# Low parts of every second unit of the down weights: an adding DMA in place of a subtraction on VectorE

## The chip, the core and the metric

The kernel runs on one core of one Trainium2 chip. The metric is the device time of one launch in microseconds (us). The kernel before takes 1096.26 us, the median of 3 runs (1096.07 to 1096.92).

Engines are named as the profile names them: PE is TensorE (matmuls; PEld is its weight load), DVE is VectorE, ACT is ScalarE, POOL is GpSimd, SP is SyncE, which here only issues DMAs.

## The reference

One encoder layer over 256 tokens of width 2048, all in float32. The change touches only its last product:

```
h = RMSNorm(x) ; p = h @ w_in                      # [256, 2048] @ [2048, 4640]
x = x + concat(attention, gated linear attention) @ w_out
u = DWConv3(RMSNorm(x) @ w_up)                     # [256, 2048] @ [2048, 11264]
x = x + (silu(u[:, :5632]) * u[:, 5632:]) @ w_down # [256, 5632] @ [5632, 2048]
```

## The kernel before, in words

Every large product is done in three passes, so that a matmul of the type float32r (a float32 that is rounded as ACT or DVE writes it) gives nearly float32 accuracy. Each operand is split in two parts: a high part `hi`, which is the operand rounded, and a low part `lo`, which is the operand less `hi`. The product is hi\*hi + hi\*lo + lo\*hi, accumulated in one PSUM bank.

Weights come in units of 512 KB, [128 partitions, 1024 columns], each of which holds two k-tiles of 512 columns in the down projection. For each unit the helper `weights` (L102 to L110) does three things: SP issues the load of the raw unit `r` (L104), ACT copies it into `hi`, rounded (L108), and DVE writes `lo = r - hi` (L109). In the down projection (L653 to L669) there are four column chunks `c` of 512 columns and in each 22 units `u`, so 88 units. A unit feeds 12 matmuls of 128x512: for two k-tiles and two tiles of tokens, `a`\*`wh` (L667), `a`\*`wl` (L668) and `b`\*`wh` (L669), where `a` and `b` are the parts of the gated activations and `wh`, `wl` are the parts of the weights. Only L668 reads the low part.

The tiles rotate through pools: 4 buffers of `raw`, 4 of `hi`, 3 of `lo`. A unit can only write into a buffer when the unit that had it last is done with it: `lo` of unit n waits for the last L668 of unit n-3, `hi` of unit n for the last L669 of unit n-4, and the load of raw unit n for the subtraction (and the copy) of unit n-4. In the profile the tiles of the down stage are named `rd`, `hd` and `ld`, and its PSUM banks `pd`.

Each engine runs its own instructions in one fixed order. A scheduler makes this order when the kernel is built, from the order of the code and a priority (`tc.high_priority`) which pulls the splits ahead; an instruction that waits holds up all that stand behind it on its engine.

Of the kernel before, what the change touches and what calls it, by code (L numbers as in the profile page):

```python
# [9 lines left out]
F32R = mybir.dt.float32r  # L10
BF16 = mybir.dt.bfloat16
U32 = mybir.dt.uint32
AF = mybir.ActivationFunctionType
ALU = mybir.AluOpType
# [3 lines left out]
A = slice(None)  # L18
P = 128
T = 256  # L20
# [7 lines left out]
EPS = 1e-6  # L28
WCOLS = 1024

# Column chunks of the input projection: (name, [(first column, width), ...], whole width).
IN_CHUNKS = [
    ("kv", [(1024, 512)], 512),
    ("qa0", [(0, 512)], 512),
# [9 lines left out]


def in_units(ci):
    """k-tiles of each weight unit of a chunk of the input projection."""
    return [1] * 4 + [2] * 6 if ci == 0 else [3] * 5 + [1] if ci in (3, 4) else [2] * 8


# Small constants and parameters, by column.
C_COS, C_SIN, C_MASK, C_MF, C_MB = 0, 256, 512, 1024, 1280
C_QG, C_QGS, C_KG, C_KGS = 1536, 1664, 1792, 1920
NCST = 2048
# [5 lines left out]
def tile_hymba_layer(  # L60
# [15 lines left out]
    nc = tc.nc  # L76
    V, S, G, PE = nc.vector, nc.scalar, nc.gpsimd, nc.tensor
# [3 lines left out]
    wp = ctx.enter_context(tc.tile_pool(name="wp", bufs=3))  # L81
# [20 lines left out]
    def weights(flat, first, cols, name):  # L102
# [6 lines left out]
            V.tensor_tensor(lo[:, :cols], r[:, :cols], hi[:, :cols].bitcast(F32), ALU.subtract)  # L109
        return hi, lo  # L110

    def split(hi, lo, src):
        S.activation(hi, src, AF.Copy)
        V.tensor_tensor(lo, src, hi.bitcast(F32), ALU.subtract)

    def product(d, a, b, start=True, stop=True):
        """d (+)= a^T b, of operands in two parts each."""
        PE.matmul(d, a[0], b[0], start=start, stop=False)
        PE.matmul(d, a[0], b[1], start=False, stop=False)
        PE.matmul(d, a[1], b[0], start=False, stop=stop)  # L120
# [1 line left out]
    def both(tiles, *index):  # L122
        return [x[index] for x in tiles]

# [1 line left out]
    g1 = pers.tile([P, NKT], F32, name="g1")  # L126
    nc.scalar.dma_start(out=g1, in_=n1)
    prm_sb = pers.tile([P, NPRM], F32, name="prm_sb")
# [11 lines left out]
        hl.append(arena([P, 8, T], F32R, f"hl{i}"))  # L140

    def load_x(kt, n):
        """n k-tiles of x, scaled by the first norm's weight and split."""
        i, o = kt // 8, kt % 8
        nc.sync.dma_start(out=xts[i][:, o : o + n], in_=xt[:, kt : kt + n])
        for j in range(n):
            with tc.high_priority(offset=1500):
                S.activation(hh[i][:, o + j], xts[i][:, o + j], AF.Copy, scale=g1[:, kt + j : kt + j + 1])
                V.scalar_tensor_tensor(
                    out=hl[i][:, o + j], in0=xts[i][:, o + j], scalar=g1[:, kt + j : kt + j + 1],  # L150
                    in1=hh[i][:, o + j].bitcast(F32), op0=ALU.mult, op1=ALU.subtract,
                )
# [46 lines left out]
    def load_wa():  # L199
        nc.sync.dma_start(out=wa_sb, in_=wa)  # L200

# [1 line left out]
    in_first = [0]  # L203

    hooks = {}
# [29 lines left out]
        with tc.high_priority(offset=1500):  # L235
            S.activation(dst, src, func, scale=rstd1[:, t : t + 1])

# [1 line left out]
    rope_kg = arena([P, 2, 1024], F32, "rope_kg")  # L239
    rope = rope_kg[:, 0].rearrange("p (a b c d) -> p a b c d", a=2, b=2, c=2)  # L240
    kg_sb = rope_kg[:, 1].rearrange("p (t c) -> p t c", t=2)
# [107 lines left out]
        if h % 2 == 1:  # L349
            split(oah[:, h - 1 : h + 1], oal[:, h - 1 : h + 1], po.rearrange("p (k s) -> p k s", k=2))  # L350

# [1 line left out]
    lr_sb = pers.tile([P, 2, 32], F32, name="lr_sb")  # L353
    gkT = arena([P, 2, GH, T], F32, "gkT")
    gh = arena([P, 2, 1024], F32R, "gh")
# [59 lines left out]
                gkT[:, 1, :, t * P : t * P + P], pq.rearrange("p (h s) -> p h s", h=GH), AF.Copy, scale=float(P) ** -0.5  # L415
            )

    # The blocks of e: for a key, -F3, the levels, B3; for a query, -B3, the levels, F3. By direction and tile of
    # tokens: (first column in the bank, role, first column in e, width, sign).
    PARTS = (  # L420
# [19 lines left out]
            V.tensor_tensor(e, e, gkT[:, role, h, t * P : t * P + P].unsqueeze(1).broadcast_to([P, 4, P]), ALU.mult)  # L440

    def mix(h):
        """The decayed products of head h: A^T [s, t] over all pairs of tokens."""
        es = arena([P, 2, 2, 4, P], F32, f"es{h}")
        scaled(h, 0, es)
        yield
        scaled(h, 1, es)
        yield

        def blk(role, t, what):  # L450
            return es[:, role, t, (0, 1 + t, 2 - t, 3)[what]]

        p1 = aux(f"p1{h}")
        p2 = aux(f"p2{h}")
        for s in range(2):
            for t in range(2):
                lv = 2 if s == t else 1
                PE.matmul(p1[:, (2 * s + t) * P : (2 * s + t + 1) * P], blk(0, s, lv), blk(1, t, lv), start=True, stop=True)
        for f in range(2):
            for t in range(2):  # L460
                PE.matmul(p2[:, (2 * f + t) * P : (2 * f + t + 1) * P], blk(0, t, 3 * f), blk(1, t, 3 - 3 * f), start=True, stop=True)
        at = work([P, 4, P], F32, f"at{h}", "sc", 3)
        S.activation(at.rearrange("p a s -> p (a s)"), p1, AF.Copy)
        diag = at[:, 0::3]
        for f, c in enumerate((C_MF, C_MB)):
            V.copy_predicated(
                diag, cst_sb[:, c : c + 256].bitcast(U32).rearrange("p (a s) -> p a s", a=2),
                p2[:, 2 * f * P : (2 * f + 2) * P].rearrange("p (a s) -> p a s", a=2),
            )
        split(atr[0][:, h], atr[1][:, h], at)  # L470
# [26 lines left out]
                PE.transpose(pt[:, e * T + t * P : e * T + t * P + P], o[:, t, e * P : e * P + P], ident)  # L497
        split(ogh[:, 2 * h : 2 * h + 2], ogl[:, 2 * h : 2 * h + 2], pt.rearrange("p (k s) -> p k s", k=2))

# [1 line left out]
    def store(ci, ps):  # L501
        """What a chunk of the projection goes to."""
        for t in range(2):
            if ci >= 8:
                c = ci - 8
                d = sg[:, t, c * 512 : c * 512 + 512]
                evac(d, ps[t], t, AF.Silu)
                dv = d.rearrange("p (h e) -> p h e", h=2)
                V.tensor_tensor(dv, dv, gn.unsqueeze(1).broadcast_to([P, 2, 256]), ALU.mult)
            elif ci == 3:  # L510
                evac(lr_sb[:, t], ps[t][:, 0:32], t)
                evac(kg_sb[:, t, 0:240], ps[t][:, 32:272], t)
            else:
                evac(
                    (kv_sb[:, t], qa_sb[:, 0, t], qa_sb[:, 1, t], None, kg_sb[:, t, 240:512],
                     gq_sb[:, t], vg[:, t, 0:512], vg[:, t, 512:1024])[ci], ps[t], t,
                )
            if ci in (6, 7):
                sl = slice((ci - 6) * 512, (ci - 5) * 512)
                split(vgr[0][:, t, sl], vgr[1][:, t, sl], vg[:, t, sl])  # L520
# [1 line left out]
    running = {}  # L522

    def go(*names):
        """Emit the next stage of each of the named pieces."""
        for name in names:
            if name not in running:
                fn = {"A": attend, "Q": queries, "M": mix, "R": retrieve}.get(name[0])
                running[name] = fn(int(name[1])) if fn else {"k": keys, "g": gates, "gk": gla_keys, "gq": gla_queries}[name]()
            next(running[name], None)  # L530
# [29 lines left out]
    for ci in range(1, len(IN_CHUNKS)):  # L560
        store(ci, project(ci))

# [1 line left out]
    x1 = [arena([P, 2, 2, 512], F32, f"x1{i}") for i in range(2)]  # L564
    xs = [arena([P, 4, 2, T], F32R, f"xs{i}") for i in range(4)]
    ssq2 = pers.tile([P, 2, 4], F32, name="ssq2")
    first = 0
    for c in range(4):
# [3 lines left out]
        for u in range(NKT // 2):  # L572
            if c == 0:
                run_hooks(10, u)
            hi, lo = weights(wo, first, 1024, f"o{c}{u}")
            first += P * 1024
            for k in range(2):
                kt = 2 * u + k
                sh, sl = (oah, oal) if kt < 8 else (ogh, ogl)
                for t in range(2):  # L580
                    a = sh[:, kt % 8, t * P : t * P + P]
                    b = sl[:, kt % 8, t * P : t * P + P]
# [9 lines left out]
        for i in range(2):  # L592
            pt = aux(f"ptx{c}{i}")
            for j in range(2):
                for t in range(2):
                    n = (2 * i + j) * P
# [18 lines left out]
    rbc = pers.tile([P, T], F32, name="rbc")  # L615
    V.tensor_copy(rbc, pb[:, :T])

# [1 line left out]
    gts = [arena([P, 2, 4, T], F32R, f"g{i}") for i in range(NFF // 4)]  # L619
    first = 0  # L620
    for f in range(NFF):
# [28 lines left out]
        S.activation(gt[:, 0, f % 4], cs[1], AF.Copy)  # L650
        V.tensor_tensor(gt[:, 1, f % 4], cs[1], gt[:, 0, f % 4].bitcast(F32), ALU.subtract)

# [1 line left out]
    first = 0  # L654
    for c in range(4):
        ps = [acc(f"pd{c}{t}") for t in range(2)]
        for u in range(NFF // 2):
            hi, lo = weights(wd, first, 1024, f"d{c}{u}")
            first += P * 1024
            for k in range(2):  # L660
                kt = 2 * u + k
                gt = gts[kt // 4]
                for t in range(2):
                    a = gt[:, 0, kt % 4, t * P : t * P + P]
                    b = gt[:, 1, kt % 4, t * P : t * P + P]
                    wh, wl = hi[:, k * 512 : k * 512 + 512], lo[:, k * 512 : k * 512 + 512]
                    PE.matmul(ps[t], a, wh, start=(kt == 0), stop=False)  # L667
                    PE.matmul(ps[t], a, wl, start=False, stop=False)  # L668
                    PE.matmul(ps[t], b, wh, start=False, stop=(kt == NFF - 1))  # L669
        x1c = x1[c // 2][:, c % 2]  # L670
        for t in range(2):
            pieces = 2 if (c, t) == (3, 1) else 1
            w = 512 // pieces
            for i in range(pieces):
                sl = slice(i * w, i * w + w)
                V.tensor_tensor(x1c[:, t, sl], ps[t][:, sl], x1c[:, t, sl], ALU.add)
                q = nc.scalar if i == 0 and pieces == 2 else nc.sync
                q.dma_start(out=out[t * P : t * P + P, c * 512 + i * w : c * 512 + i * w + w], in_=x1c[:, t, sl])
# [39 lines left out]


def _units(w, sizes):  # L720
    """[K, n] -> units of a few k-tiles, each [128 partitions, k-tiles * n] in one run."""
    n, k, parts = w.shape[1], 0, []
    for per in sizes:
        parts.append(w[k : k + per * P].reshape(per, P, n).transpose(1, 0, 2).reshape(-1))
        k += per * P
    return np.concatenate(parts)
# [54 lines left out]
```

## Time and profile before

| what | value |
|---|---|
| median of 3 runs | 1096.26 us (1096.07 to 1096.92) |
| profiled execution: span from first to last instruction | 1094.4 us |
| PE busy, whole span | 1080.4 us (99%) |
| DVE busy, whole span | 783.6 us (72%) |
| ACT busy, whole span | 529.7 us (48%) |
| POOL busy, whole span | 31.2 us (3%) |
| HBM read | 199.89 MB |

The profiled execution's own time is its span of 1094.4 us; the launch adds some 1.9 us around it, if the profiled execution was like the median one (1096.26 - 1094.4). Matmuls are pipelined, so the 389 ns that the profile gives for one overlap: the next starts some 0.227 us after it. Busy shares are over the whole span; a stage is judged by rows of that stage alone. The down stage runs from about 851 us to 1090 us. The profile's line numbers are those of the kernel before; in the changed kernel all lines below L110 stand 13 lower, so that L667 to L669 are there L680 to L682.

### The profile page before, as it was taken

Reading aid. Unit: us, or ns where it says so; the run is one execution under the profiler, and the core shown is the slowest. Engines: PE = TensorE matmul, PEld = TensorE weight load, DVE = VectorE, ACT = ScalarE, POOL = GpSimd, SP = SyncE. Lnnn points to the kernel's source line nnn. Section 1 sums busy time; section 2 is a strip of 40 time slices with the busy share of each in tenths; the row PEclk is TensorE's granted clock in tenths of the full one; section 3 lists DMA queues with packets and bytes.
Section 4 is the critical chain, followed back from the end, with each engine's and each line's share of the span. In section 5 each row is a group of like instructions: output and inputs, shape, how many; then the busy total and the mean of one; then the engine's idle time right before and its main releaser. Section 6 shows DMA issues by size and latency. Waiting matters only on the chain.

```text
span 1094.4 us, 14985 instructions
## 1 busy us (share of the span) xinstructions
PE 1080.4 (99%) x5616; PEld 921.1 (84%) x5616; DVE 783.6 (72%) x1173; ACT 529.7 (48%) x780; POOL 31.2 (3%) x24
## 2 busy tenths in 40 slices
PE   7899999999999999999999999999999999999998
PEld 6789888888888888888888888888888888888886
DVE  7788777756555888888888888888888544444443
ACT  6345566764445544444444444444444433333331
POOL 4311000010000000000000000000000000000000
PEclk9999999999999999999999999999999999999999
DMA  8565544436556655655565565555565656666662
GB/s 302 173 201 165 165 154 148 139 117 187 201 194 219 200 184 184 191 186 184 189 186 184 189 187 182 190 190 179 189 191 181 195 195 210 196 214 196 210 193 79
DMA packets 58040, 202.96 MB, mean 185 GB/s; under 512 B 6576, under 2 KB 7600, under 8 KB 57840
## 3 DMA queue, kind: packets, MB, share of 16 engines
q1 hardware_dynamic: 57680, 201.87, 58.2%
q8 instruction: 44, 0.72, 0.3%
q14 instruction: 28, 0.23, 0.1%
q10 hardware_dynamic: 288, 0.14, 0.0%
HBM read 199.89 MB, written 2.10 MB: 185 GB/s over the span
## 4 chain that ended last, share of the span: by engine, by line
PE 97%; DVE 1%; DMA 1%; ACT 0%; issue 0%; SPq 0%; DVEq 0%; ACTq 0%
PE pu L632 30%; PE pu L633 15%; PE pd L667 7%; PE pd L669 7%; PE pd L668 7%; PE po L586 3%; PE po L584 3%; PE po L585 3%; PE pvg L228 1%; PE pvg L229 1%; PE pqa L229 1%; PE pgt L230 1%; PE pgt L228 1%; PE pvg L230 1%; PE pqa L230 1%; PE pgt L229 1%
## 5 line engine op out<-in xcount | busy, mean ns | idle before, releaser
L632 PE MATMUL pu<-xs,hu 128*128 128x512 f32 x1408 | 497.4, 399 | 0.0
L633 PE MATMUL pu<-xs,lu 128*128 128x256 f32 x1408 | 395.3, 281 | 0.0
L632 PEld LDWEIGHTS pu<-xs,hu 128*128 128x128 f32 x1408 | 264.4, 188 | 65.7
L108 ACT ACTIVATE hu<-ru 128x1024 fp32r<-128x1024 f32 x176 | 186.9, 1062 | 253.0 <-PE pu L632 145.6
L633 PEld LDWEIGHTS pu<-xs,lu 128*128 128x128 f32 x1408 | 266.0, 189 | 0.2
L109 DVE TENSOR_TENSOR lu<-ru,hu 128x1024 fp32r<-128x1024 f32 x176 | 215.3, 1224 | 47.4 <-PE pu L633 41.2
L109 DVE TENSOR_TENSOR ld<-rd,hd 128x1024 fp32r<-128x1024 f32 x88 | 107.8, 1225 | 117.5 <-PE pd L668 112.2
L108 ACT ACTIVATE hd<-rd 128x1024 fp32r<-128x1024 f32 x88 | 93.6, 1064 | 143.8 <-PE pd L669 136.7
L668 PE MATMUL pd<-ld,g 128*128 128x512 f32 x352 | 136.9, 389 | 0.0
L667 PE MATMUL pd<-hd,g 128*128 128x512 f32 x352 | 136.9, 389 | 0.0
L669 PE MATMUL pd<-hd,g 128*128 128x512 f32 x352 | 136.9, 389 | 0.0
L669 PEld LDWEIGHTS pd<-hd,g 128*128 128x128 f32 x352 | 66.1, 188 | 13.8
L668 PEld LDWEIGHTS pd<-ld,g 128*128 128x128 f32 x352 | 66.1, 188 | 13.6
L667 PEld LDWEIGHTS pd<-hd,g 128*128 128x128 f32 x352 | 66.1, 188 | 13.6
L109 DVE TENSOR_TENSOR lo<-ro,ho 128x1024 fp32r<-128x1024 f32 x32 | 39.0, 1224 | 36.3 <-ACT ho L108 23.8
L108 ACT ACTIVATE ho<-ro 128x1024 fp32r<-128x1024 f32 x32 | 33.9, 1061 | 44.5 <-DMA ro<-in_wo_dram 30.7
L636 DVE TENSOR_TENSOR u<-u,pu 128x256 f32<-128x256 f32 x88 | 37.0, 421 | 13.8 <-ACT u L635 13.3
L643 DVE SCALAR_TENSOR_TENSOR c<-u,prm_sb,c 128x255 f32<-128x255 f32 x88 | 42.5, 484 | 3.0
L640 DVE SCALAR_TENSOR_TENSOR c<-u,prm_sb,c 128x255 f32<-128x255 f32 x88 | 42.0, 478 | 0.1
L639 DVE TENSOR_SCALAR c<-u,prm_sb 128x256 f32<-128x256 f32 x88 | 36.2, 412 | 3.0
L637 DVE TENSOR_TENSOR u<-u,rbc 128x256 f32<-128x256 f32 x88 | 37.1, 422 | 1.5
L635 ACT ACTIVATE u<-pu 128x256 f32<-128x256 f32 x88 | 32.1, 365 | 0.0
(225 smaller groups left out, 1425.7 us busy)
## 6 DMA issues: line engine op xcount, KB each, us to landing
ru<-in_wu_dram SPq DMA_DIRECT2D x176, 512.0 KB, 3.5
rd<-in_wd_dram SPq DMA_DIRECT2D x88, 512.0 KB, 3.9
ro<-in_wo_dram SPq DMA_DIRECT2D x32, 512.0 KB, 3.6
riqa<-in_wi_dram SPq DMA_DIRECT2D x16, 512.0 KB, 4.1
rivg<-in_wi_dram SPq DMA_DIRECT2D x16, 512.0 KB, 3.5
rigt<-in_wi_dram SPq DMA_DIRECT2D x16, 512.0 KB, 3.5
riqg<-in_wi_dram SPq DMA_DIRECT2D x8, 512.0 KB, 4.0
rilk<-in_wi_dram SPq DMA_DIRECT2D x10, 408.0 KB, 3.6
```

What stands on the lines that cost most here:

```text
L108: S.activation(hi[:, :cols], r[:, :cols], AF.Copy)
L109: V.tensor_tensor(lo[:, :cols], r[:, :cols], hi[:, :cols].bitcast(F32), ALU.subtract)
L632: PE.matmul(pu, wh, x2, start=(u == 0 and k == 0), stop=False)
L633: PE.matmul(pu[:, T:], wl, x2[:, :T], start=False, stop=(u == 1 and k == 7))
L636: V.tensor_tensor(ut, ut, pu[:, :T], ALU.add)
L637: V.tensor_tensor(ut, ut, rbc, ALU.mult)
L639: V.tensor_scalar(c, ut, cw[:, 1, n : n + 1], cb[:, n : n + 1], op0=ALU.mult, op1=ALU.add)
L640: V.scalar_tensor_tensor(out=c[:, 1:T], in0=ut[:, 0 : T - 1], scalar=cw[:, 0, n : n + 1], in1=c[:, 1:T], op0=ALU.mult, op1=ALU.add)
L643: V.scalar_tensor_tensor(out=c[:, 0 : T - 1], in0=ut[:, 1:T], scalar=cw[:, 2, n : n + 1], in1=c[:, 0 : T - 1], op0=ALU.mult, op1=ALU.add)
L667: PE.matmul(ps[t], a, wh, start=(kt == 0), stop=False)
L668: PE.matmul(ps[t], a, wl, start=False, stop=False)
L669: PE.matmul(ps[t], b, wh, start=False, stop=(kt == NFF - 1))
```

## The change

Units with an even `u` go through `weights` as before. Units with an odd `u` (44 of the 88) go through a new helper, `weights_added`: the raw unit is loaded as before; ACT writes the rounded unit with its sign turned into `lo` (one more activation), and the rounded unit into `hi`; then a DMA that POOL issues reads the raw unit a second time from DRAM and adds it to what stands in `lo`. DVE does nothing for these units. The other edits of the diff drop comments and docstrings and are left out here.

```
+    def weights_added(flat, first, cols, name):
+
+        src = flat[first : first + P * cols].rearrange("(p c) -> p c", p=P)
+        r = raw(f"r{name}")
+        nc.sync.dma_start(out=r[:, :cols], in_=src)
+        hi = wp.tile([P, WCOLS], F32R, name=f"h{name}", tag="hi", bufs=4)
+        lo = wp.tile([P, WCOLS], F32R, name=f"l{name}", tag="lo")
+        with tc.high_priority(offset=1500):
+            S.activation(lo[:, :cols], r[:, :cols], AF.Copy, scale=-1.0)
+            S.activation(hi[:, :cols], r[:, :cols], AF.Copy)
+            G.dma_start(out=lo[:, :cols], in_=src, accum_op=ALU.add)
+        return hi, lo
...
-            hi, lo = weights(wd, first, 1024, f"d{c}{u}")
+            hi, lo = (weights_added if u % 2 else weights)(wd, first, 1024, f"d{c}{u}")
```

The scheduler's order changes on ACT, DVE, POOL and PE. On ACT in the middle of the first column chunk (`hd010` is the high part of chunk 0, unit 10; `ld011` the low part of unit 11; `rd` the raw units), before:

```order
L108 ACTIVATE hd010_8209<-rd010_8207 128x1024
L108 ACTIVATE hd011_8227<-rd011_8225 128x1024
L108 ACTIVATE hd012_8245<-rd012_8243 128x1024
L108 ACTIVATE hd013_8263<-rd013_8261 128x1024
```

and after:

```order
L108 ACTIVATE hd010_8214<-rd010_8212 128x1024
L121 ACTIVATE hd011_8232<-rd011_8230 128x1024
L120 ACTIVATE ld011_8233<-rd011_8230 128x1024
L108 ACTIVATE hd012_8251<-rd012_8249 128x1024
L121 ACTIVATE hd013_8269<-rd013_8267 128x1024
L120 ACTIVATE ld013_8270<-rd013_8267 128x1024
```

The negated copy of an odd unit stands behind that unit's own high part and ahead of the high part of the next even unit. On POOL, which has nothing in this stage before, the last of its earlier work is followed by the adding DMAs, one for each odd unit and in their order:

```order
L182 TENSOR_TENSOR rstd2_3160<-isq_3162,mhalf_87 128x2
L122 DMA ld01_8048<-in_wd_dram 128x1024
L122 DMA ld03_8085<-in_wd_dram 128x1024
L122 DMA ld05_8122<-in_wd_dram 128x1024
L122 DMA ld07_8159<-in_wd_dram 128x1024
```

On PE the first matmuls of an odd unit (here unit 3 of chunk 0; `pd00` and `pd01` are the banks of the two tiles of tokens, `g1` the activations), before:

```order
L667 MATMUL pd00_8025<-hd03_8083,g1_3175 128x512
L668 MATMUL pd00_8025<-ld03_8084,g1_3175 128x512
L669 MATMUL pd00_8025<-hd03_8083,g1_3175 128x512
L667 MATMUL pd01_8026<-hd03_8083,g1_3175 128x512
L668 MATMUL pd01_8026<-ld03_8084,g1_3175 128x512
```

and after:

```order
L680 MATMUL pd00_8025<-hd03_8084,g1_3175 128x512
L680 MATMUL pd01_8026<-hd03_8084,g1_3175 128x512
L681 MATMUL pd00_8025<-ld03_8085,g1_3175 128x512
L682 MATMUL pd00_8025<-hd03_8084,g1_3175 128x512
L681 MATMUL pd01_8026<-ld03_8085,g1_3175 128x512
```

Two matmuls instead of one now stand ahead of the first that reads the low part. The rest of the unit, and all even units, keep their order.

## Rows read from the trace of the kernel before

**Rows 1.** The page: its span, and the busy time of each engine

```profile
span 1094.4 us, 14985 instructions
PE 1080.4 (99%) x5616; PEld 921.1 (84%) x5616; DVE 783.6 (72%) x1173; ACT 529.7 (48%) x780; POOL 31.2 (3%) x24
```

**Rows 2.** Windows of the down stage: busy, clock, DMA share, GB/s; last without splits

```profile
core 0: us, PE busy (x) PEld busy (x) DVE busy (x) ACT busy (x) POOL busy (x), PEclk, DMA share, GB/s
851.00:1083.00 232.00, 232.00 (x1026) 192.13 (x1025) 111.64 (x99) 91.20 (x88) 0.00 (x0) 1.00 0.62 194
1083.20:1089.80 6.60, 6.60 (x31) 5.45 (x29) 0.27 (x1) 0.00 (x0) 0.00 (x0) 1.00 0.00 0
```

**Rows 3.** Groups of the down stage: busy, mean ns | idle before, releaser

```profile
L109 DVE TENSOR_TENSOR ld<-rd,hd 128x1024 fp32r<-128x1024 f32 x83 | 101.7, 1225 | 116.3 <-PE pd L668 112.0 <-issue 2.4 <-PE pd L669 1.8
L108 ACT ACTIVATE hd<-rd 128x1024 fp32r<-128x1024 f32 x82 | 87.3, 1064 | 135.0 <-PE pd L669 135.0
```

**Rows 4.** Timeline, two units of the down stage: start, us, engine, what [idle before]

```profile
951.07 0.39 PE L669 MATMUL pd<-hd,g 128*128 128x512 f32 x1
...
951.29 0.39 PE L667 MATMUL pd<-hd,g 128*128 128x512 f32 x1
...
951.32 1.22 DVE L109 TENSOR_TENSOR ld<-rd,hd 128x1024 fp32r<-128x1024 f32 x1 [1.50 <-PE pd L668]
951.49 1.06 ACT L108 ACTIVATE hd<-rd 128x1024 fp32r<-128x1024 f32 x1 [1.66 <-PE pd L669]
...
954.01 0.39 PE L667 MATMUL pd<-hd,g 128*128 128x512 f32 x1
...
956.73 0.39 PE L667 MATMUL pd<-hd,g 128*128 128x512 f32 x1
...
956.96 0.39 PE L668 MATMUL pd<-ld,g 128*128 128x512 f32 x1
...
957.18 0.39 PE L669 MATMUL pd<-hd,g 128*128 128x512 f32 x1
```

**Rows 5.** Last subtraction of the stage, and first and last matmul of the last unit

```profile
1081.88 1.23 DVE L109 TENSOR_TENSOR ld<-rd,hd 128x1024 fp32r<-128x1024 f32 x1 [1.49 <-PE pd L668]
...
1087.29 0.39 PE L667 MATMUL pd<-hd,g 128*128 128x512 f32 x1
...
1089.79 0.39 PE L669 MATMUL pd<-hd,g 128*128 128x512 f32 x1
```

**Rows 6.** Loads of the down stage (L104): issue ns min/median/max, us to landing

```profile
L104 SPq DMA_DIRECT2D rd<-in_wd_dram x79: 327/328/328, 860.1 to 1072.3; - x79
...
DMA to landing us min/median/max: 3.3/4.1/5.1
```

**Rows 7.** Windows of the first 40 us, columns as in the other windows

```profile
5.00:10.00 5.00, 4.43 (x17) 3.02 (x16) 3.16 (x7) 3.05 (x7) 0.00 (x0) 1.00 0.93 324
10.00:15.00 5.00, 2.92 (x13) 1.84 (x11) 4.00 (x4) 4.31 (x8) 3.27 (x1) 1.00 1.01 369
15.00:20.00 5.00, 3.53 (x9) 2.84 (x10) 5.00 (x7) 4.44 (x8) 1.56 (x2) 0.66 1.05 398
```

**Rows 8.** DMA issues of the first 30 us: KB each, median us to landing

```profile
rikv<-in_wi_dram SPq DMA_DIRECT2D x6, 512.0 KB, 5.1
```

**Rows 9.** Timeline of POOL: its last instruction

```profile
356.41 0.70 POOL L169 TENSOR_TENSOR rstd<-isq,mhalf 128x2 f32<-128x2 f32 x1 [117.77 <-DVE isq L168]
```

## The prediction

> **What bounds the kernel now.** I read the engines' busy times first, then the windows of the stage that the change touches, then who waits there for whom, and last the timeline of a few units. PE is busy for 1080.4 of 1094.4 us [rows 1]. In the down stage it has no gap at all: 232.00 of 232.00 us, at a granted clock of 1.00, the 2.4 GHz level [rows 2]. ACT and DVE there wait for PE and not PE for them: DVE is idle for 112.0 us until an L668 of PE frees a buffer of `lo`, ACT for 135.0 us until an L669 frees one of `hi` [rows 3]. So the subtraction that the change removes is work that is already hidden.
>
> The timeline gives the cadence. Units start on PE at 951.29, 954.01 and 956.73, so 2.72 us each, 12 matmuls of 0.227 us; one pair of an even and an odd unit takes 5.44 us [rows 4]. At 951.32 a buffer of `lo` has come free and DVE begins the subtraction for the unit that starts at 956.73. That it is this unit is seen at the end of the stage: the last subtraction starts at 1081.88 and the last unit at 1087.29, again 5.41 us apart [rows 5].
>
> **What is removed.** 44 subtractions of 1.225 us, 53.9 us of DVE [rows 3]. No other engine waits for DVE here, so they return nothing. Could PE's matmuls be slowed by DVE's and ACT's traffic? After the last split, PE runs 12 matmuls from 1087.29 to about 1090.02 (1089.79 + 0.23), 2.73 us [rows 5], with 0.27 us of DVE and none of ACT beside it [rows 2]: the same 2.72 us. The most that the change can gain is therefore about nothing.
>
> **What is added on ACT.** 44 activations of 1.064 us, 46.8 us, against 135.0 us of idle time [rows 3]. Two activations of an odd unit and one of an even make 3.2 us in a pair of 5.44. The high part of the next even unit stands behind the negated copy and comes up to 1.06 us later; it is written almost three units (8 us) ahead of its use, so that costs nothing. The negated copy waits for the same buffer as the subtraction did, and that high part, whose own buffer comes free 0.17 us later (951.49) [rows 4], is the only thing that it holds up. DVE and the raw buffers of the odd units are released at about the same moment as before, so SP's loads stay where they are.
>
> **What is added on PE.** No instruction; the first reader of an odd unit's low part comes one matmul (0.23 us) later.
>
> **What is added on the DMA engines and POOL: the term that decides.** 44 adding DMAs of 512 KB. Before, `lo` was ready 1.23 us after its buffer came free. Now it is ready after ACT's copy and then a whole round trip of a DMA. The time there is for it: the buffer is free at 951.32; the first reader would stand at 957.18 (the place of the L669 behind 956.96 in [rows 4], since two L680 now stand ahead); that is 5.86 us, less 1.06 us of ACT, so **4.80 us** from the end of the negated copy to the low part landed, everything in between included. I call the time that the round trip needs D.
>
> If D is longer, PE waits x in each odd unit. Between the buffer's release and the reader lie the odd unit before it, which has a wait x of its own, one even unit, and the wait x of the unit itself. So 4.80 + 2x = D, and x = (D - 4.80) / 2: two adding DMAs may be under way at once, so that each late microsecond is shared by two units.
>
> D is not in the trace, since POOL issues no DMA before; its last instruction is at 356.41 [rows 9]. I build it from the loads:
> - A plain load of 512 KB lands 4.1 us after its issue in this stage (3.3 to 5.1) [rows 6]. The engines' own time for it, when they are full: at shares of 1.01 and 1.05 they moved 369 and 398 GB/s [rows 7], mean 384, so 524,288 bytes take 1.37 us. The fixed rest is 4.1 - 1.37 = 2.73 us.
> - An addition has to read two things, the unit from DRAM and what stands in `lo`. I count two passes, 2.74 us.
> - Loads share the engines with it. One load is due in 2.72 us; in the 4 to 5 us in which the addition has the engines, one or two come between. I take 1.5 times 1.37 = 2.05 us.
> - POOL's issue: the nearest row is its shortest instruction, 0.70 us [rows 9], against 0.33 us for an issue on SP [rows 6]: 0.37 us more.
>
> D = 2.73 + 2.74 + 2.05 + 0.37 = 7.89 us, x = 1.55 us, times 44 = **68 us**.
>
> The bounds of D. From below: a plain load's 4.1 + 0.37 = 4.47 us, under 4.80, no wait at all. From above by latency: two loads one after the other with engines that are full, 2 x 5.1 [rows 8] + 0.37 = 10.57 us, x = 2.9, 127 us. From above by the engines' time, where a byte added costs r copies: a pair needs (2 + r) x 1.37 us of the engines. At r = 2 that is 5.48, against a pair of 5.44 + 1.55 = 6.99 in the forecast, so latency decides; at r = 4 it is 8.22 us, 2.78 over 5.44, 122 us; at r = 4.7 it is 9.18 us, 164 us. I take the middle of the latency's ends, since the share of 0.62 that the engines have now [rows 2] leaves no room for a second read and a second pass without loads landing later than now.
>
> The Trainium skill, page "DMA: Bandwidth & Descriptors", section "Anatomy of one DMA — SWDGE (gpsimd) path", gives a DMA that POOL issues 2.0 us plus its bytes at 436 GB/s. That would be an estimate of 3.2 us for 512 KB, or 4.4 us for two passes, both under 4.80: no change. The row of this case speaks against so low a figure: plain loads land after 4.1 us here, 0.9 above it [rows 6]. The page "Collectives: The Full Stack", section "The bandwidth ceiling: the fold count and why AG ≠ RS ≠ AR", speaks against the change: an add that the DMA engines do needs two source reads through the same ring and ran at half the rate of a copy. No row here shows an addition.
>
> **The sum.** Profiled execution 1094.4 us [rows 1], + 68 us - 0 = 1162; the median of the runs stands 1.9 us above the span, so about **1164 us**. The own range of this case (D from 5.3 to 10.57) is 1107 to 1223 us.
>
> **Rivals.**
> - *Hidden (not slower).* D stays at or under 4.80 us. For it: plain loads land at 4.1, and the engines have 0.38 of their time free [rows 2, 6]. Against it: only 0.33 us are left over 4.47 for what a second read and a second pass of half of the units do to all the other transfers. Time 1096 us, within 0.2% of now. The page's 4.4 us would lead here.
> - *The engines' time decides.* An addition costs three copies or more, so that DMA and no longer PE sets the pace of a pair: r = 3 gives 6.85 us, +62; r = 4 +122; r = 6 gives 10.96 us, +243. For it: the engines' share of 0.62 is already high for 194 GB/s [rows 2], so small a margin is soon gone. Against it: none that a row shows. It differs from the forecast in that the DMA share would stand near 1. I give it 1200 to 1340, most likely 1220 us.
> - *The clock.* PE's waits let the granted clock fall. In the first 20 us a stretch of 5 us with 2.92 us of matmuls was followed by one at 0.66 (part of it at 1.2 GHz), one with 4.43 us was followed by 1.00 [rows 7]. In the forecast PE would work 5.44 of 6.99 us, which lies between, so the rows don't decide. At 1.2 GHz a pair takes 10.9 us and hides any D up to some 10; if half of the stage of 239 us ran so, +120: 1216 us.
> - *Faster.* Nothing in the stage can give time back, as worked out above. A chance of 0.02 is left for what the trace doesn't show.
>
> **How the numbers follow.** Forecast (latency, 1107 to 1223) 0.50, hidden 0.12, engines' time 0.30, clock 0.06, faster 0.02. The bound of what a measurement tells from no change is 0.2%, 2.2 us. Faster 0.02, same 0.12, slower 0.86. The range: 1096 takes in the hidden case; 1260 takes in the engines' case up to r = 4.7 (1096 + 164), and half of the clock's; above are the dearer additions, about 0.14, and below the 0.02.
>
> **What would show it.** Right: PE with gaps in the down stage alone, one in each odd unit, ahead of its first matmul that reads `ld`, of about 1.5 us; their releaser the adding DMA; its landing 7 to 9 us after the issue; DVE's and ACT's groups with 44 subtractions fewer and 44 activations more at the same 1.06 us; the clock at 1.00; HBM reads up by 44 x 0.52 = 23 MB to 223 MB; the stages before 851 us as they were. Hidden would be seen by landings under 4.8 us and no gaps. The engines' case shows a DMA share over 0.95 and loads on SP that land late too, ACT waiting for `rd`. The prediction is wrong if PE waits for something else (the negated copy held up on ACT, a POOL queue that needs microseconds for an issue), or if the gaps come at places other than odd units.

## The result and the profile after

The changed kernel takes 1190.03 us (median of 4 runs, 1186.48 to 1205.10), the kernel before 1096.59 us beside it (also 4 runs). The longest run, 1205.10 us, fell in a slower state of the chip, so the ratio leaves it out; the median of the other three is 1188.06 us. The ratio is 1.0836, 95% interval 1.082 to 1.0852: about 92 us slower. The forecast was 1164 us, 68 us slower; the range of 1096 to 1260 holds the time. The profiled execution is the one of 1186.48 us; its span is 1184.7 us, 90.3 more than before.

The page: the span, the engines' busy times, and the DMA queues (packets, MB, share of 16 engines; q1 are the loads of SP, q0 the adding DMAs).

```profile
span 1184.7 us, 15034 instructions
PE 1107.5 (93%) x5616; PEld 930.5 (79%) x5616; DVE 730.2 (62%) x1129; ACT 570.7 (48%) x824; POOL 68.5 (6%) x68
...
q1 hardware_dynamic: 57680, 201.87, 53.8%
q0 software_dynamic: 6336, 23.07, 11.3%
...
HBM read 222.96 MB, written 2.10 MB: 190 GB/s over the span
```

Against [rows 1], DVE has lost 53.4 us (44 subtractions), ACT has won 41.0 and POOL 37.3 us, and HBM reads grew by 23.07 MB, as they should. PE shows 27.1 us more for the same 5616 matmuls. That can't be more work, so matmuls ran slower, or part of the waits is counted as theirs.

The down stage, from the first to the last L682 (the third pass; L669 before) in a listing of that line, was 238.7 us (851.1 to 1089.8) and is now 328.7 us, 90.0 more. Before and after:

```profile
L669 PE MATMUL pd<-hd,g x352: 388/389/389, 851.1 to 1089.8; 128*128 128x512 f32 x176
```

```profile
L682 PE MATMUL pd<-hd,g x352: 387/389/632, 851.3 to 1180.0; 128*128 128x512 f32 x176
```

It begins where it began, so all of the loss is here. All stage lengths below are read in this way. Its window (columns as in [rows 2]), and the groups of the low parts with their idle time:

```profile
851.00:1180.00 329.00, 265.80 (x1055) 207.56 (x1055) 60.13 (x57) 131.50 (x130) 37.99 (x44) 0.94 0.84 208
```

```profile
L681 PE MATMUL pd<-ld,g 128*128 128x512 f32 x352 | 148.3, 421 | 63.2 <-DMA ld<-in_wd_dram 63.2
...
L120 ACT ACTIVATE ld<-rd 128x1024 fp32r<-128x1024 f32 x43 | 45.5, 1059 | 63.3 <-PE pd L681 63.3
```

PE, which had no gap here [rows 2], is idle for 63.2 us, all of it ahead of L681 and released by the adding DMA. The rest of the 90 us, 26.8, is PE time, most of it matmuls stretched at a clock of 0.94; how much of the loss the clock makes is a question for e_fill below. ACT behaves as forecast: it waits for PE to free the buffer, as DVE did [rows 3].

The time from issue to landing, for all loads of the odd units and for the adding DMAs (us, minimum, median, maximum; before [rows 6] 3.3/4.1/5.1):

```profile
DMA to landing us min/median/max: 3.5/5.2/9.3
```

```profile
L122 POOL DMA_DIRECT2D ld<-in_wd_dram x44: 863/872/1056, 850.4 to 1172.3; - x44
...
DMA to landing us min/median/max: 5.5/8.0/9.5
```

The addition lands after 8.0 us. One round trip in the timeline:

```profile
948.35 1.06 ACT L120 ACTIVATE ld<-rd 128x1024 fp32r<-128x1024 f32 x1 [1.78 <-PE pd L681]
...
949.70 0.87 POOL L122 DMA_DIRECT2D ld<-in_wd_dram  x1 [10.44 <-ACT ld L120]
...
953.79 1.06 ACT L120 ACTIVATE ld<-rd 128x1024 fp32r<-128x1024 f32 x1 [1.10 <-PE pd L681]
953.82 0.61 PE L680 MATMUL pd<-hd,g 128*128 128x512 f32 x2
...
957.82 0.50 PE L681 MATMUL pd<-ld,g 128*128 128x512 f32 x1 [3.39 <-DMA ld<-in_wd_dram]
```

The negated copy ends at 949.41; POOL starts 0.29 us later; the reader starts at 957.82. So D is 8.41 us here. Over all 44 additions the same 0.29 us and the median landing of 8.0 make 8.3 us. The next unit's copy starts at 953.79 while PE still waits: two additions are under way, as the forecast had it.

### The profile page after: what moved, and what is told of

The parts are those of the page before. It is cut to its first block, busy times and chain, and to the rows that moved or that the text cites. A ratio compares the mean times of both kernels' runs of the same rounds, so it can differ in the third digit from the quotient of the medians.

```text
span 1184.7 us, 15034 instructions
## 1 busy us (share of the span) xinstructions
PE 1107.5 (93%) x5616; PEld 930.5 (79%) x5616; DVE 730.2 (62%) x1129; ACT 570.7 (48%) x824; POOL 68.5 (6%) x68
## 3 DMA queue, kind: packets, MB, share of 16 engines
q0 software_dynamic: 6336, 23.07, 11.3%
## 4 chain that ended last, share of the span: by engine, by line
PE 70%; issue 22%; DMA 3%; POOL 3%; DVE 1%; ACT 0%; POOLq 0%; DVEq 0%; SPq 0%; ACTq 0%
PE pu L645 27%; PE pu L646 14%; POOL ld L122 3%; DMA ld<-in_wd_dram 3%; PE po L599 2%; PE po L598 2%; PE po L597 2%; PE pvg L241 1%; PE pvg L242 1%; PE pqa L242 1%; PE pgt L243 1%; PE pgt L241 1%; PE pvg L243 1%; PE pqa L243 1%; PE pgt L242 1%
## 5 line engine op out<-in xcount | busy, mean ns | idle before, releaser
L645 PE MATMUL pu<-xs,hu 128*128 128x512 f32 x1408 | 497.4, 399 | 0.0
L645 PEld LDWEIGHTS pu<-xs,hu 128*128 128x128 f32 x1408 | 264.4, 188 | 65.7
L109 DVE TENSOR_TENSOR ld<-rd,hd 128x1024 fp32r<-128x1024 f32 x44 | 53.9, 1225 | 255.7 <-PE pd L681 253.6
L681 PE MATMUL pd<-ld,g 128*128 128x512 f32 x352 | 148.3, 421 | 63.2 <-DMA ld<-in_wd_dram 63.2
L682 PE MATMUL pd<-hd,g 128*128 128x512 f32 x352 | 144.3, 410 | 0.0
L681 PEld LDWEIGHTS pd<-ld,g 128*128 128x128 f32 x352 | 70.5, 200 | 91.5 <-DMA ld<-in_wd_dram 76.9
L680 PE MATMUL pd<-hd,g 128*128 128x512 f32 x352 | 134.9, 406 | 0.0
L122 POOL DMA_DIRECT2D ld<-in_wd_dram x44 | 38.5, 876 | 776.0 <-ACT c L660 491.8
L682 PEld LDWEIGHTS pd<-hd,g 128*128 128x128 f32 x352 | 70.6, 200 | 14.4
L680 PEld LDWEIGHTS pd<-hd,g 128*128 128x128 f32 x352 | 69.6, 198 | 15.5
L120 ACT ACTIVATE ld<-rd 128x1024 fp32r<-128x1024 f32 x44 | 46.6, 1058 | 63.3 <-PE pd L681 63.3
```

The costliest lines, as they stand in the source:

```text
L120: S.activation(lo[:, :cols], r[:, :cols], AF.Copy, scale=-1.0)
L122: G.dma_start(out=lo[:, :cols], in_=src, accum_op=ALU.add)
L645: PE.matmul(pu, wh, x2, start=(u == 0 and k == 0), stop=False)
```

## The experiments

Theory L is the forecast: the round trip D against the 3 buffers of `lo`. Theory E is the rival of the engines' time, theory C that of the clock. Behind each time stand, in brackets, its ratio to the kernel before and the 95% interval. I call *room* the time from the end of the negated copy to the first reader when PE doesn't wait, 4.80 us in the forecast.

**Everything but the wait** (e_shadow). The additions go into spare tiles that nothing reads:

```
+            V.tensor_tensor(lo[:, :cols], r[:, :cols], hi[:, :cols].bitcast(F32), ALU.subtract)
+            spare = wp.tile([P, WCOLS], F32R, name=f"s{name}", tag="spare", bufs=2)
+            S.activation(spare[:, :cols], r[:, :cols], AF.Copy, scale=-1.0)
+            G.dma_start(out=spare[:, :cols], in_=src, accum_op=ALU.add)
```

> All the work of the change (44 negated copies on ScalarE, 44 adding DMAs from GpSimd), but into spare tiles that nothing reads; the low parts come from VectorE as before. To make room there are 3 raw buffers instead of 4 and a scratch tile shares another's buffers. Theory L (the round trip of the adding DMA against 3 buffers of lo): nobody waits for the additions, so 1096 to 1101 us. Theory E (the DMA engines' time: two loads of 1.66 us and an addition of 3.04 us by their packets make 6.4 us for a pair of units that PE needs 5.44 us for): the loads come late, ScalarE waits for rd, and the time is about 1138 us (1125 to 1190).

Measured 1143.56 us (ratio 1.0426, 1.0369 to 1.0483), which is E's number and not L's. It is E's in part by chance: about 11 of the 47 us lie ahead of the down stage, which begins at 862.4. In the stage ACT waits for the loads:

```profile
ACT hd L108 <- DMA rd<-in_wd_dram: 59.0, 20, 5.2
ACT sd L123 <- DMA rd<-in_wd_dram: 56.2, 34, 4.7
```

But it has 3 raw buffers, which has to be taken out. **e_raw3** is the kernel before with that alone:

```
-        return wp.tile([P, WCOLS], F32, name=name, tag="raw", bufs=4)
+        return wp.tile([P, WCOLS], F32, name=name, tag="raw", bufs=3)
```

> The kernel before with 3 raw buffers instead of 4 and the smaller scratch tiles of e_shadow and e_lo5, nothing else. Theories L and E: 1096 to 1099 us, so that what e_shadow lost is due to the additions' use of the DMA engines. Rival B (fewer raw buffers made the loads late in e_shadow): over 1110 us, up to 1143.

Measured 1108.30 us (1.0102, 1.008 to 1.0124), neither the theories' nor the rival's number. Its down stage is the 238.7 us of before; it begins 16.0 us later (867.1), so the loss is ahead of it. The stage of e_shadow is 273.3 us, 34.6 longer: with 3 raw buffers the loads, slowed by the additions, come too late. How much of that 4 raw buffers hide, the last pair below tells.

**The copies on ACT alone** (e_dve_add).

```
-            G.dma_start(out=lo[:, :cols], in_=src, accum_op=ALU.add)
+            V.tensor_tensor(lo[:, :cols], r[:, :cols], lo[:, :cols].bitcast(F32), ALU.add)
```

> The negated copy on ScalarE stays, but VectorE adds the raw unit onto it instead of a DMA. Theories L and E: 1096 to 1098 us, since the low part is ready 2.3 us after its buffer came free and no DMA is added. Rival A (the copies on ScalarE or their place in its order cost something of their own): over 1100 us, with PE waiting for ld.

Measured 1097.24 us (1.0001, 0.9992 to 1.0011), stage 238.7 us, PE without a gap at 40 us more of ACT:

```profile
851.00:1083.00 232.00, 232.00 (x1027) 192.22 (x1026) 111.75 (x99) 131.53 (x131) 0.00 (x0) 1.00 0.62 195
```

Neither the 44 activations nor the reads of a negated copy cost anything.

**A copy in place of the addition** (e_plain): the same call without `accum_op`.

> The DMA from GpSimd copies the raw unit over the negated copy instead of adding to it, so the low parts of the odd units are wrong. Theory L: the round trip is shorter by the second read. With a landing near 5 to 5.5 us and 1.2 us from the end of the copy to the end of the issue, D is about 6.0 to 6.5 us, 22 times (D - 4.8) is 26 to 37 us: 1122 to 1134 us. Theory E: 3 times 1.66 is 5.0 us per pair, under 5.44: 1096 us. Rival Q (GpSimd's queue and its issue cost the time, whatever the DMA does): 1180 to 1190 us as in the changed kernel.

Measured 1121.43 us (1.0228, 1.0213 to 1.0243), stage 261.8 us. The queue and the landing in its page, then the additions' own line:

```profile
q0 software_dynamic: 6336, 23.07, 5.9%
...
ld<-in_wd_dram POOLq DMA_DIRECT2D x44, 512.0 KB, 4.7
...
L122 POOL DMA_DIRECT2D ld<-in_wd_dram x44: 537/537/755, 851.1 to 1107.1; - x44
...
DMA to landing us min/median/max: 3.7/4.7/7.3
```

This lies just under L's 1122 to 1134 us, and far from E's 1096 and from Q's 1180 to 1190. 22 x (D - 4.80) = 23.1 would give D = 5.85 us, but that is no trip of this trace: the median one is 0.29 + 4.7 = 5.0 us, hardly over the room, and a few long landings, up to 7.3 us, make the waits. Of the 90 us, about 67 come with the adding. A packet took 5.9% of 16 x 1118.4 us over 6336, 167 ns; an adding one 11.3% of 16 x 1184.7 over 6336, 338 ns: twice.

**Fewer additions** (e_quarter): `u % 4 == 3` in place of `u % 2`.

> Only every fourth unit (u % 4 == 3, 20 of 88) goes through the adding DMA. Theory L: an addition now has its wait to itself, x = D - 4.8 instead of half of it, so with D of 8 to 8.8 us 20 times 3.2 to 4.0, 64 to 80 us: 1160 to 1176 us, nearly the cost of 44 additions. If D shrinks to 7 with less traffic, 44 us, 1140 us. Theory E: 4 loads and an addition are 9.7 us of the engines for 10.9 us of PE: 1096 us. Rival N (each addition costs the same, 90 us / 44 = 2.05 us): 1137 us.

Measured 1195.30 us (1.0913, 1.0886 to 1.0941). Twenty additions cost more than 44. N and E are out. L forecast nearly the cost of 44 (each now bears its whole lateness), 64 to 80 us, but the stage is 96.5 us longer:

```profile
L682 PE MATMUL pd<-hd,g x352: 386/390/632, 851.4 to 1186.6; 128*128 128x512 f32 x176
...
L122 POOL DMA_DIRECT2D ld<-in_wd_dram x20: 863/872/1056, 855.0 to 1173.4; - x20
...
DMA to landing us min/median/max: 5.5/7.9/8.5
```

Additions land after 7.9 us here, at a DMA share of about 0.6, so it isn't the other traffic that makes D so long. The rest, by theory C, is the clock. After a gap of 3.24 us, matmuls soon follow at a distance of 0.42 to 0.43 us:

```profile
963.01 0.80 PE L681 MATMUL pd<-ld,g 128*128 128x512 f32 x1 [3.24 <-DMA ld<-in_wd_dram]
963.61 0.63 PE L682 MATMUL pd<-hd,g 128*128 128x512 f32 x1
964.03 0.63 PE L681 MATMUL pd<-ld,g 128*128 128x512 f32 x1
964.46 0.63 PE L682 MATMUL pd<-hd,g 128*128 128x512 f32 x1
```

The window behind it is busy throughout, at a granted clock of 0.64, so part of it at 1.2 GHz:

```profile
965.00:970.00 5.00, 5.00 (x16) 3.97 (x15) 1.22 (x1) 1.06 (x1) 0.00 (x0) 0.64 0.10 19
```

**e_quarter_fill** fills the gap:

```
+                    if u % 4 == 3 and k == 0 and t == 0:
+                        for _ in range(12):
+                            PE.matmul(fill, a, wh, start=True, stop=True)
```

> e_quarter (1195.3 us) with 12 matmuls of 128x512 more in each of the 20 units with an addition, into a PSUM bank that nothing reads. The order puts them ahead of the first matmul that reads the added low part, so they run in the wait of 3.0 us (12 times 0.227 are 2.72 us). Theory C (the gap lets the granted clock fall and the matmuls behind it run at 1.2 GHz, which costs about 38 us of e_quarter's 98): the clock stays near 1.00 and the time falls to 1160 to 1170 us, 20 times (D - 4.8) with D of 8.2 to 8.5. Rival (the clock's loss is hidden in the round trip, or is none): 1190 to 1200 us. Rival (extra matmuls cost their time): 1195 + 20 times 2.72 = 1250 us.

Measured 1166.36 us (1.0629, 1.0608 to 1.0651), stage 307.1 us (the third pass is L686 here and in e_fill):

```profile
L686 PE MATMUL pd<-hd,g x352: 388/389/402, 853.2 to 1160.3; 128*128 128x512 f32 x176
...
851.00:951.00 100.00, 97.67 (x428) 79.14 (x427) 32.36 (x34) 38.50 (x40) 6.26 (x7) 1.00 0.66 191
```

Theory C holds: 240 matmuls more and 28.1 us less in the stage (335.2 to 307.1). What stays, 68.4 us, is 20 x 3.42, so D = 8.22, which is also what the trace has, 0.29 and a landing of 7.9. The same in the changed kernel (**e_fill**, 6 for each odd unit):

> The changed kernel with 6 matmuls of 128x512 more for each odd unit, into a PSUM bank that nothing reads; the scheduler's order puts 12 of them (2.72 us) into every second odd unit, ahead of the first matmul that reads the added low part, which is where the changed kernel waits for 3 to 4 us. Theory L with C (a round trip D of 8.4 us, and the clock falls in the gaps): without the clock's fall 22 times (8.4 - 4.8) are 80 us, 1172 to 1180 us, the clock near 1.00. Theory L without C: 1186 to 1192 us. If the extra matmuls cost their time: 1190 + 60 = 1250 us.

Measured 1174.41 us (1.0701, 1.0673 to 1.0728), the clock at 1.00:

```profile
L686 PE MATMUL pd<-hd,g x352: 388/389/402, 844.0 to 1165.6; 128*128 128x512 f32 x176
...
851.00:951.00 100.00, 95.76 (x412) 76.77 (x413) 18.45 (x16) 42.23 (x42) 11.32 (x13) 1.00 0.88 219
```

The number is that of L with C, but only half of it for that reason: the stage is 321.6 us, 7.1 less than in the changed kernel; some 8 us more were won in the up stage, which this build ran faster (last section). So the clock costs some 7 us of the 90, and L 82.9: D = 4.80 + 82.9 / 22 = 8.57. The 7 us are the difference of two single executions, and the runs of either kernel spread over 5 to 6 us, so they are a rough figure. They are less than the 26.8 us of longer PE time in the changed kernel, since slow matmuls that run while an addition is under way stand, by the chain of the forecast, where PE would have waited; how much of the loss they would make without that is not measured.

**More buffers of `lo`.** e_lo4 has 4 of them (`tag="lo", bufs=4`), e_lo5 has 5 and 3 raw buffers.

> The changed kernel with 4 buffers of lo instead of 3 (a scratch tile of earlier stages shares another's buffers to make room). The round trip then has 4.80 + 2.72 = 7.52 us. Theory L alone: 2x = D - 7.5 with D of 8.4 to 9.0, 44 times 0.45 to 0.75: 1116 to 1130 us. Theory L with theory E behind it (once the wait is short, the DMA engines' time of 6.2 to 6.5 us a pair sets the pace, as in e_shadow): 1135 to 1150 us, the DMA share above 0.9 and ScalarE waiting for rd. Theory E alone: as the changed kernel, 1186 to 1192 us.

> The changed kernel with 5 buffers of lo and 3 raw buffers instead of 4. The round trip has 10.2 us, more than its 8.4 to 9.0. Theory L alone: 1096 to 1102 us. Theory L with E behind it: 1135 to 1150 us, as e_shadow (1143.6) and no better than with 4 buffers by more than 10 us.

Measured 1109.34 us (1.0101, 1.0082 to 1.012) and 1137.99 us (1.038, 1.0357 to 1.0403), stages 256.9 and 269.9 us. One buffer more takes 71.8 of the 90 us back: L decides the changed kernel. (The total of e_lo4 is under both forecasts for it, because its up stage was some 9 us faster too, see the last section; with them it would be 1118 us, in the range of L alone.) But e_lo4's 18 us left could be L's (44 x (8.3 - 7.52) / 2 = 17) or E's, and e_lo5 has the fault of 3 raw buffers. In e_lo4 the engines are full:

```profile
L682 PE MATMUL pd<-hd,g x352: 388/389/402, 842.5 to 1099.4; 128*128 128x512 f32 x176
...
851.00:951.00 100.00, 95.95 (x413) 76.29 (x412) 22.57 (x20) 52.80 (x53) 15.34 (x18) 1.00 1.00 273
```

**e_lo4_plain** takes the adding out:

> e_lo4 (1109.3 us, DMA share 1.00) with a plain copy by GpSimd instead of the addition, so the low parts of the odd units are wrong. A copy lands after 4.7 us, well under the 7.5 us that 4 buffers give. Theory E (the 11 us that e_lo4 has left are the full DMA engines): the share falls to 0.8 and the time to 1096 to 1099 us. Rival (something else of the path: GpSimd's issue, the third reader of DRAM, ScalarE's order): 1105 to 1110 us as e_lo4.

Measured 1096.30 us (0.9999, 0.9989 to 1.0009). The total fits E, but the stage of 246.5 us is still 7.8 longer, and the total hides it behind a faster up stage. The copies land after 7.0 us in the median here and up to 8.5, so some trips are longer than 7.52 us, and PE does wait for them (3.7 us at L681): the run doesn't tell E from L. The last pair has 5 buffers and all 4 raw ones, with and without the addition:

```
-        pT = work([P, 2, 2, T], F32R, f"pT{h}", "pT")
+        pT = work([P, 2, 2, T], F32R, f"pT{h}", "pT", 1)
...
-            ut = work([P, T], F32, f"u{n}", "pT")
+            ut = work([P, T], F32, f"u{n}", "pT", 1)
```

> The changed kernel with 5 buffers of lo and all 4 raw buffers; the room comes from one scratch buffer less in the up stage and in the attention, so the down stage is read by itself (from its first to its last L682; 238.7 us before, 328.7 in the changed kernel, 256.9 in e_lo4). Theory L alone (5 buffers give the round trip 10.2 us, D is 8.4): 239 to 243 us. Theory E behind it (the DMA engines are full at a share of 0.98 in e_lo4): 250 to 260 us, as e_lo4, share 0.95 or more.

> The same with a plain copy by GpSimd instead of the addition, so the low parts of the odd units are wrong. Theories L and E: a down stage of 239 to 243 us at a share of 0.8 to 0.9. If it stays at e_lo4_plain's 246.5 us or above, something of the path that is neither the round trip nor the addition costs time.

Measured 1100.30 us (1.0037, 1.0022 to 1.0052), stage 251.8 us; and 1087.69 us (0.9919, 0.9902 to 0.9935), stage 238.7 us. Their windows, first with the addition, then with the copy:

```profile
945.00:1045.00 100.00, 97.50 (x423) 78.33 (x421) 23.40 (x21) 52.18 (x51) 14.46 (x17) 1.00 1.01 286
```

```profile
945.00:1045.00 100.00, 100.00 (x443) 82.84 (x442) 24.46 (x22) 56.36 (x55) 10.16 (x19) 1.00 0.91 298
```

With the addition 13.1 us stay, at a share of 1.01; the copy, with as many bytes from DRAM, has none at 0.91. Both stages are as L with E behind it forecast them. But the 13 us are not E's alone, since five buffers don't give the room of 10.2 us on which both expectations rest. The run with the copy, where PE never waits, shows the room:

```profile
942.64 1.06 ACT L108 ACTIVATE hd<-rd 128x1024 fp32r<-128x1024 f32 x1 [1.60 <-PE pd L682]
...
943.61 1.04 ACT L120 ACTIVATE ld<-rd 128x1024 fp32r<-128x1024 f32 x1
...
953.55 0.39 PE L681 MATMUL pd<-ld,g 128*128 128x512 f32 x1
```

The negated copy no longer waits for a buffer of `lo`, but it stands on ACT behind a high part that waits for one of the 4 buffers of `hi` (L682). It ends at 944.65, and its reader starts at 953.55: a room of 8.90 us. The additions of e_lo5_raw4 land after 8.6 us, so with the 0.29 about half of the trips are as long as that; and some of its copies start late, because ACT waits for a load:

```profile
DMA to landing us min/median/max: 5.5/8.6/9.5
...
ACT ld L120 <- DMA rd<-in_wd_dram: 15.6, 11, 4.2
PE pd L681 <- DMA ld<-in_wd_dram: 8.0, 12, 1.8
```

By its timeline PE is idle for 8.2 us ahead of L681. Of these, 3.9 us lie in four units whose copy started late behind its load (E), and 4.3 us in units whose trip was itself longer than the room (L, with landings of 8.6 where the changed kernel has 8.0). So E is there behind L, but no run gives its price by itself; 13 us is what both leave.

## Why the prediction was right, and where it was off

- *The subtraction removed returns nothing, and ACT's copies cost nothing.* Right: e_dve_add at 1.0001.
- *The deciding term is the round trip against 3 buffers of `lo`.* Right, and shown: a fourth buffer takes back 71.8 of 90.0 us of the stage.
- *x = (D - 4.80) / 2, shared by two units.* Right as a sum: with 44 additions it gives D = 8.57 (e_fill), with 20, each for itself, 8.22 (e_quarter_fill), and the trace has 8.3 in the median. As a picture it was off: the forecast had a gap of 1.5 us in each odd unit. There are 32 gaps of over 0.05 us ahead of L681 in the profile, between 0.19 and 4.97 us, some runs of them even and some with 3.4 us in one odd unit and none in the next. The chain fixes only the sum of two neighbouring waits.
- *D = 7.89 us.* The mis-sized term. The landing alone took 8.0 us in the median, and the 0.29 us from ACT's end to POOL's start, which the sum didn't have, come on top: 8.3 read from the trace, 8.22 to 8.57 worked back from the stages. That is 0.3 to 0.7 us in D, 7 to 15 us in the time. By parts, a trip with a plain copy, 4.47 us in the forecast, is 5.0 in the median of e_plain, and the addition adds 3.3 us to it, where the sum had 3.42 (1.37 for a second pass and 2.05 for loads between). That the last figure came so near is partly luck: the second pass and the one and a half loads were counts without a row, and no run separates them. POOL's issue, taken at 0.70 us [rows 9], takes 0.87 for an addition and 0.54 for a copy. The "middle of the latency's ends" is 7.52 and not 7.89, which is the sum's.
- *The clock at 1.00.* Wrong. It was a rival with 0.06; it is a term: 7 us in the changed kernel, 28 in e_quarter. It isn't a case that excludes the forecast, as it was set up, but a surcharge behind long gaps: the window from 940 to 945, in which a wait of 3.56 us ends, was at 0.50, which is 1.2 GHz.

```profile
940.00:945.00 5.00, 4.21 (x10) 3.34 (x11) 0.00 (x0) 0.00 (x0) 0.00 (x0) 0.50 1.02 269
```

- *Sum:* 68 forecast + 7 to 15 for D + 7 for the clock = 82 to 90, against 90.0 in the profiled execution. By the median trip of 8.3 us the sum is 84, and 6 us stay open. Both errors point the same way.
- *The engines' time.* Not what decides: the share is 0.84, and a buffer more, which gives the engines no less to do, takes most of the loss back. It is there behind L (loads land after 5.2 us instead of 4.1), at a price that no run isolates; L and E together leave 13 us in e_lo5_raw4.
- *Rules of the Trainium skill.* The Trainium skill, page "DMA: Bandwidth & Descriptors", section "Anatomy of one DMA — SWDGE (gpsimd) path", gave an estimate of 3.2 us for a copy and 4.4 us for two passes; measured from issue to landing, with loads of SP beside them, are 4.7 and 8.0, so it would have led to "hidden", and the measurement decides. The Trainium skill, page "Collectives: The Full Stack", section "The bandwidth ceiling: the fold count and why AG ≠ RS ≠ AR", has an add run at half the rate of a copy. The packets here agree, 338 against 167 ns.

## What to carry to other kernels

A low part that a DMA makes has to be judged by its round trip against the buffers of its tile, not by the idle shares of the engines: count the time from the buffer's release to its first reader, and if the trip is longer, buy a buffer before anything else. Then look at what the copy ahead of the trip waits for: the fourth buffer of `lo` gave 2.7 us of room, the fifth only 1.4, since a buffer of `hi` came to stand in the way. No number of buffers makes this change pay here, because the subtraction that it removes cost nothing. Thinning such transfers out need not help, since late ones that lie on one chain share their lateness. And a gap on PE can cost more than its length, since the clock may fall behind it: the 20 gaps of e_quarter, most of them of 3 us and more, cost 28 us beyond their own time.

## What was not expected of the hardware

- 20 additions cost more than 44: the ratios are 1.0913 and 1.0836. About 28 us of the loss of e_quarter are the clock.
- In the up stage, which no edit meant to touch, the same matmuls run at two speeds, by the build. The group of L645 (L632 before; busy us, mean ns) in the changed kernel, and then in e_lo5_raw4_plain:

```profile
L645 PE MATMUL pu<-xs,hu 128*128 128x512 f32 x1408 | 497.4, 399 | 0.0
```

```profile
L645 PE MATMUL pu<-xs,hu 128*128 128x512 f32 x1408 | 488.4, 394 | 0.0
```

The stage from the first to the last of them is 498.3 us in the kernel before and in the changed one, and 489.2 in the other. That is why e_lo5_raw4_plain, whose down stage is no shorter than before, takes 8.9 us less in all (with low parts that are wrong). The faster group (489 to 493 us) has e_shadow, e_lo4, e_lo4_plain, e_lo5, both e_lo5_raw4, e_raw3 and e_fill in it; all but e_fill have other tile sizes or counts in SBUF, and e_quarter_fill, with the same extra bank as e_fill, is in the slower one. The cause stays open. The kernel before with the tiles of e_lo5_raw4, to which these numbers point as faster than both, was not tried.
